# Storing attention outputs untransposed, adding their two shares by DMA, and normalising the stored rows later, in a hybrid attention and retention layer

## The chip, the cores and the metric

The kernel runs on one core of a Trainium2 chip, in float32. The metric is the device time of one launch in microseconds (us). Five engines work side by side, each on its own queue of instructions in order: TensorE (PE; its weight loads are shown as PEld), VectorE (DVE), ScalarE (ACT), GpSimd (POOL) and SyncE (SP), which here only issues DMAs. ScalarE and GpSimd issue DMAs too.

## What is computed

One layer on 1024 latent tokens (a grid of 16 rows by 64 columns) and 256 context tokens, width 1024. After adaptive normalisation one projection feeds two branches: neighbourhood attention with 8 heads of 64, and a two-way chunked retention with 4 heads. Both are projected, gated, merged, and followed by an output projection and a convolutional MLP. The part that matters here is the attention's output and its way into the projection:

```python
s_loc = jnp.einsum('bhqd,bhiqjd->bhqij', q_row, k_win) + bias[None]
...
s_ctx = jnp.einsum('bhqd,bhcd->bhqc', q_row, kc)
p = jax.nn.softmax(jnp.concatenate([s_loc, s_ctx], axis=-1).astype(jnp.float32), axis=-1).astype(v.dtype)
...
return (jnp.einsum('bhqij,bhiqjd->bhqd', p_loc, v_win)
        + jnp.einsum('bhqc,bhcd->bhqd', p_ctx, vc))
...
merged = jax.nn.sigmoid(gate_na) * (o_na @ w_proj_na) + jax.nn.sigmoid(gate_ret) * (o_ret @ w_proj_ret)
```

## The kernel before, in words

**Arithmetic.** Matmul operands are split into a high and a low part (float32r), and a product is the sum of three matmuls: high x high, high x low, low x high. `split` (lines 88 to 90) makes the parts: a cast on ScalarE, a subtraction on VectorE. `chain` (lines 105 to 117) runs such products and yields after every few matmuls, so that its caller can put them in pieces between other work.

**Order of the work.** The program is written engine by engine in program order; a scheduler with a model of durations then fixes the order on each engine, taking earlier lines first where several are ready, so that later work moves up into gaps. What is wrapped in `late` keeps its program order on its engine. Buffers come from pools: a tile with `bufs=n` has n places, and a new one waits until an old one is no longer used.

**Attention (80 to 376 us of the profile).** Heads are taken in 4 pairs, the queries of a pair in 8 blocks of 128 (a block is 16 grid rows by 8 columns, so tokens are stored grouped by block): 32 units. The loop over units overlaps three steps of neighbouring units. For unit i it issues `scores` (lines 470 to 490): eight matmuls, the maxima on VectorE, the exponentials with their sums on ScalarE, the reciprocals of the sums on VectorE into the unit's small tile `st`. For unit i-1 it transposes the probabilities on TensorE (`ptp`, lines 498 and 505), splits them (`PT`), and multiplies them with the values (`R`, line 516). The values stand as high and low columns, so `R` holds, for each head, 64 rows of the high values' share and 64 rows of the low values' share, with queries along the free axis; lines 518 and 519 add the shares of the probabilities' two parts into `rs`. For unit i-2 `output` (lines 522 to 531) transposes `rs` per head (`tq`), scales and adds the two value shares with the reciprocal (ACT line 528, DVE line 529) into `oq`, with queries as rows, and stores it by one SyncE DMA. Between these steps stand pieces of the next pairs' projections and of gate matmuls (`piece`), which fill TensorE's waits. With each unit GpSimd issues a DMA that prepares sums of weights (`puts`, line 587, and lines 555 and 559).

**Retention (376 to 690 us).** Four heads, each with 2 context blocks and 8 token blocks. A slot (`slot`) does one block's projection for one head (`front`, `turn`, `state`) and one mixing step of the head before (`mix_a`, `mix_b`, `mix_c`). `mix_a` splits the states, the high part on ScalarE (line 1203) and the low part on GpSimd (line 1204), and TensorE needs both. GpSimd goes on issuing the weight-sum DMAs, one or two a slot. SyncE loads the heads' weights (line 94) into a few buffers.

**Start of the merge (from 690 us).** SyncE loads the attention's rows back (`onr`, line 1366), 8 loads of 128 tokens by 512 channels. TensorE transposes them (`tpn`, line 1371, 32 transposes), ScalarE and VectorE split the result into `ona` (lines 1373 and 1374), and the projection `pn` (`mm_a` over `ona`, lines 113 to 115) follows, whose result is gated and stored. Beside it GpSimd and VectorE form sums of the normalised input for later gate matmuls (`b`, lines 1354 and 1357), in buffers that they share with `onr` (10 places).

The later parts, gates, output projection and MLP, are not touched.

Of the kernel before, what the change touches and what calls it, by code (L numbers as in the profile page):

```python
# [8 lines left out]
F32 = mybir.dt.float32  # L9
# [7 lines left out]
P = 128  # L17
# [8 lines left out]
NJ = 8  # L26
# [14 lines left out]
def tile_hybrid_layer(ctx, tc: tile.TileContext, io, dbg=None):  # L41
# [7 lines left out]
        return tc.alloc_tile_pool(name=name, bufs=bufs, side=side, space=PSUM, reuse_waits="tile")  # L49

    dram = tc.alloc_tile_pool(name="dram", bufs=1, space=DRAM)
    d_ona = dram.tile([GR, NJ, 8, NPAIR * P], F32, name="d_ona")
    d_oret = dram.tile([RH * 2, P, T], F32, name="d_oret")
    d_x1 = dram.tile([T, D], F32, name="d_x1")
    d_ada = dram.tile([32, P], F32, name="d_ada")
    d_s = dram.tile([6, 4, P, 512], F32, name="d_s")
    d_g = dram.tile([8, 4, P, 512], F32, name="d_g")
# [23 lines left out]
    pool.memset(mhalf, -0.5)  # L81

    col = cpool.tile([P, 48], F32, name="col")


    wpool = sb("wstream", "left")
# [41 lines left out]
    def perm(ap, c):  # L128
        return ap.rearrange("p (j r c) -> p r j c", j=NJ, c=c)
# [328 lines left out]
    class Unit:  # L458
# [8 lines left out]
        def scores(self):  # L467
            j, nl, nt, k0, pair = self.j, self.nl, self.nt, self.g0 * P, self.pair
            boff = 0 if j == 0 else (640 if j == NJ - 1 else 256)
            sl = [pna.tile([P, 512], F32, tag="sl", bufs=2, name="sl") for _ in range(2)]  # L470
            sc = pna.tile([P, 2, 512], F32, tag="sc", bufs=1, name="sc")[:, :, :C]
            self.st = st = na.tile([P, 16], F32, tag="st", bufs=3, name="st")
            self.Pm = Pm = [na.tile([P, 640], F32, tag="P", bufs=2, name="P") for _ in range(2)]
            for h in range(2):
                q = pair.qS[h][:, j * P : (j + 1) * P]
                k, kl = pair.kH[h], pair.kL[h]
                pe.matmul(sl[h][:, :nl], q, k[:, k0 : k0 + nl], start=True, stop=False)
                pe.matmul(sl[h][:, :nl], q, kl[:, k0 : k0 + nl], start=False, stop=True)
                pe.matmul(sc[:, h], q, k[:, T:NK], start=True, stop=False)
                pe.matmul(sc[:, h], q, kl[:, T:NK], start=False, stop=True)  # L480
            for h in range(2):
                vec.tensor_tensor_reduce(out=Pm[h][:, :nl], in0=sl[h][:, :nl], in1=pair.bias[h][:, boff : boff + nl], op0=ALU.add, op1=ALU.max, scale=1.0, scalar=NEG, accum_out=st[:, h : h + 1])
            vec.tensor_reduce(st[:, 2:4], sc, op=ALU.max, axis=AX.X)
            vec.tensor_tensor(st[:, 4:6], st[:, 0:2], st[:, 2:4], ALU.max)
            vec.tensor_scalar(st[:, 6:8], st[:, 4:6], -1.0, None, ALU.mult)
            for h in range(2):
                act.activation(Pm[h][:, :nl], Pm[h][:, :nl], AF.Exp, bias=st[:, 6 + h : 7 + h], scale=1.0, accum_out=st[:, 8 + h : 9 + h])
                act.activation(Pm[h][:, nl:nt], sc[:, h], AF.Exp, bias=st[:, 6 + h : 7 + h], scale=1.0, accum_out=st[:, 10 + h : 11 + h])
            vec.tensor_tensor(st[:, 12:14], st[:, 8:10], st[:, 10:12], ALU.add)
            vec.reciprocal(st[:, 14:16], st[:, 12:14])  # L490

        def transp(self, part):
            if part == 0:
# [17 lines left out]
        def values(self):  # L511
            R = pna.tile([P, 2, 2 * P], F32, tag="pt", bufs=2, name="R")
            for h in range(2):
                for c in range(self.nch):
                    g = self.g0 + c if c < self.ng else NJ + c - self.ng
                    pe.matmul(R[:, h], self.pair.V[:, g, h].rearrange("p a b -> p (a b)"), self.PT[h][:, c].rearrange("p a b -> p (a b)"), start=c == 0, stop=c == self.nch - 1)  # L516
            self.rs = rs = na.tile([P, 2, P], F32, tag="rs", bufs=1, name="rs")
            act.copy(rs, R[:, :, P : 2 * P])
            vec.tensor_tensor(rs, R[:, :, 0:P], rs, ALU.add)

        def output(self):
            tq = pna.tile([P, 4, 2, HD], F32, tag="pt", bufs=2, name="tq")
            for h in range(2):
                pe.transpose(tq[:, h].rearrange("p a b -> p (a b)"), self.rs[:, h], ident)
            oq = na.tile([P, 2, HD], F32, tag="oq", bufs=2, name="oq")
            for h in range(2):
                r = self.st[:, 14 + h : 15 + h]
                act.activation(oq[:, h], tq[:, h, 1], AF.Copy, scale=r)
                vec.scalar_tensor_tensor(oq[:, h], tq[:, h, 0], r, oq[:, h], ALU.mult, ALU.add)
            pr = self.pair.pr  # L530
            sync.dma_start(d_ona[:, self.j, :, pr * P : (pr + 1) * P], oq.rearrange("p a b -> p (a b)"))

    def ada_load():
        w = na.tile([P, D], F32, tag="aw", bufs=2, name="aw")
# [117 lines left out]
    with tc.manual_schedule():  # L652
# [302 lines left out]
        for shape, dt, tag, bufs in (  # L955
            ([P, 896], F32, "bias", 2),
            ([P, 16], F32, "st", 3),
            ([P, 640], F32, "P", 2),
            ([P, NJ + NCB, 2, 2, HD], F32R, "V", 1),
            ([P, 5, 2, P], F32R, "PT", 2),  # L960
            ([P, 2, P], F32, "rs", 1),
            ([P, 2, HD], F32, "oq", 2),
            ([P, 512], F32, "gs", 1),
        ):
            na.tile(shape, dt, tag=tag, bufs=bufs, name=tag)
# [77 lines left out]
        next(pieces, None)  # L1043

    us = []
    for i in range(NPAIR * NJ + 2):
        live = i < NPAIR * NJ
        u1 = us[i - 1] if 1 <= i <= NPAIR * NJ else None
        u2 = us[i - 2] if i >= 2 else None
# [12 lines left out]
        if u1:  # L1062
            u1.transp(1)
        if live:
            pair = pairs[i // NJ]
            if i % NJ == 0 and i:
                pair.load_bias()
            us.append(Unit(pair, i % NJ))
            us[i].scores()
        if u2:  # L1070
            u2.output()
        if u1:
            u1.values()
            puts(gate_sums, u1.st[:, 14:15], 1)
        piece()
        piece()
    for _ in pieces:
        pass
    pna.release()
    na.release()  # L1080
    csp.release()
# [7 lines left out]
    Dm = rc.tile([P, RH, P], F32, name="Dm")  # L1089

    def decay_masks():
        dtab = rt.tile([P, 4, P], F32, tag="dtab", bufs=1, name="dtab")
        sync.dma_start(dtab, io["dtab"])
        for h in range(RH):
            f, b = lg[:, 0, h : h + 1], lg[:, 1, h : h + 1]
            e1 = rt.tile([P, P], F32, tag="A0", bufs=1, name="e1")
            act.activation(e1, dtab[:, 0], AF.Exp, scale=f)
            act.activation(Dm[:, h], dtab[:, 1], AF.Exp, scale=b)
            vec.scalar_tensor_tensor(e1, e1, RKS, dtab[:, 2], ALU.mult, ALU.mult)
            vec.scalar_tensor_tensor(Dm[:, h], Dm[:, h], RKS, dtab[:, 3], ALU.mult, ALU.mult)  # L1100
            vec.tensor_tensor(Dm[:, h], Dm[:, h], e1, ALU.add)
# [161 lines left out]
            return self.n >= NTB + 2  # L1263


    def slot(main, mix, head=None, i=None):
        def step():
            next(main, None)
# [22 lines left out]


    mix, last = None, (None, None)
    for h in range(RH):
# [51 lines left out]
    d_onat = d_ona.rearrange("r j c d -> (r j c) d")  # L1346


    def hx_sums(k):
# [11 lines left out]
        yield  # L1361

    onr = []
    for n in range(KB):
        raw = g_raw("onr")
        sync.dma_start(raw, d_onat[n * P : (n + 1) * P])
        onr.append(raw)
    for n, raw in enumerate(onr):
        tp = pg.tile([P, NPAIR, P], F32, tag="g", bufs=6, name="tpn")
        for k in range(NPAIR):  # L1370
            pe.transpose(tp[:, k], raw[:, k * P : (k + 1) * P], ident)
        dst = [ona[w][:, :, n * P : (n + 1) * P] for w in range(2)]
        act.copy(dst[0], tp)
        vec.tensor_tensor(dst[1], tp, dst[0].bitcast(F32), ALU.subtract)


    def open3(out, ah, al, bh, bl, first, last):
# [741 lines left out]
```

## Time and profile before

| | us |
|---|---|
| median of 3 runs (1734.2 to 1735.79) | 1734.36 |
| the profiled execution, first to last instruction | 1733.2 |
| TensorE busy in it | 1717.1 |
| VectorE busy in it | 1222.2 |
| ScalarE busy in it | 839.6 |
| GpSimd busy in it | 540.4 |

The profile gives for each engine the time in which it was busy; a matmul's end is modelled, so matmuls overlap and a busy TensorE need not be at its peak. A row of a view names a source line, an engine, an operation, what is written from what, and a count. A wait row names the instruction that waited, what it waited for, and then the total, the count and the longest. The chain of work that ended last is followed back from the last instruction, at each step to what released it, or to the instruction before it on its engine. SPq and ACTq rows are DMA issues on SyncE and ScalarE. Issue rows of the DMA view end with the size and the median time from issue to landing; queue rows give packets, MB, and the time of their packets as a share of 16 DMA engines over the span.

### The profile page before, as it was taken

The numbers are of one execution on the slowest core, as the hardware profiler recorded it, in microseconds if no ns is written. First come the engines' busy times: TensorE is split into PE (matmuls) and PEld (weight loads), VectorE is DVE, ScalarE is ACT, GpSimd is POOL, SyncE is SP. The second block draws the span as 40 slices with busy tenths as digits, with TensorE's granted clock in tenths as the row PEclk, the third lists the DMA queues.
The fourth block names the chain that finished last, engine by engine and source line by source line (L and its number), as shares of the span: only waits on it lengthen the run. The fifth ranks groups of instructions, "written<-read, shape, count | busy, mean of one in ns | idle before, by whom it ended". The sixth has DMA issues, their size and how long they took to land.

```text
span 1733.2 us, 25367 instructions
## 1 busy us (share of the span) xinstructions
PE 1717.1 (99%) x8552; PEld 1435.8 (83%) x8552; DVE 1222.2 (71%) x2461; ACT 839.6 (48%) x1796; POOL 540.4 (31%) x706
## 2 busy tenths in 40 slices
PE   9999999999999999999999999999999999999997
PEld 7788888888888888888888888788788888888886
DVE  5778787665676766855555657867888889856756
ACT  6566666563453434543444333644444444545444
POOL 2100000002334343512223121012667667311444
PEclk9999999999999999999999999999999999999999
DMA  9344455532231223588975656768666776998744
GB/s 378 95 138 143 141 158 160 151 118 64 68 101 37 77 46 109 180 273 256 277 241 201 217 184 181 272 216 230 172 165 179 196 192 168 261 313 294 242 153 175
DMA packets 142002, 313.04 MB, mean 181 GB/s; under 512 B 19152, under 2 KB 32112, under 8 KB 135664
## 3 DMA queue, kind: packets, MB, share of 16 engines
q1 hardware_dynamic: 117536, 230.40, 38.6%
q0 software_dynamic: 12032, 70.27, 18.1%
q10 hardware_dynamic: 12304, 10.75, 1.8%
q8 instruction: 67, 1.10, 0.2%
q14 instruction: 63, 0.52, 0.1%
HBM read 250.78 MB, written 121.91 MB: 215 GB/s over the span
## 4 chain that ended last, share of the span: by engine, by line
PE 81%; issue 5%; DMA 5%; DVE 5%; POOL 2%; ACT 2%; SPq 0%; POOLq 0%; ACTq 0%; DVEq 0%
PE u L1379 28%; PE mm L126 4%; PE mm L124 4%; PE mm L125 4%; PE mm L115 4%; PE mm L114 4%; PE mm L113 4%; PE y L1379 2%; PE R L516 2%; DMA ur<-d_a 2%; PE pr L114 2%; PE pr L113 2%; PE pr L115 2%; PE ptp L498 2%; PE om L125 1%
## 5 line engine op out<-in xcount | busy, mean ns | idle before, releaser
L1379 PE MATMUL u<-T,wc 128*128 128x512 f32 x960 | 225.3, 390 | 0.7 <-ACT pu L1413 0.5
L1379 PEld LDWEIGHTS u<-T,wc 128*128 128x128 f32 x960 | 179.4, 188 | 40.9 <-ACT pu L1413 3.7
L1379 PE MATMUL y<-wc,ahl 128*128 128x512 f32 x924 | 210.1, 389 | 0.4 <-DVE wc L90 0.4
L1379 PEld LDWEIGHTS y<-wc,ahl 128*128 128x128 f32 x924 | 173.3, 188 | 36.8 <-DVE wc L90 0.8
L90 DVE TENSOR_TENSOR wc<-ur,wc 128x512 fp32r<-128x512 f32 x161 | 119.2, 743 | 62.6 <-ACT wc L89 60.8
L89 ACT CAST wc<-ur 128x512 fp32r<-128x512 f32 x161 | 99.7, 621 | 117.7 <-PE u L1379 74.1
L114 PE MATMUL mm<-low,wc 128*128 128x512 f32 (+1 forms) x312 | 118.9, 381 | 0.0
L1379 PE MATMUL u<-h2a,wc 128*128 128x512 f32 x480 | 113.1, 390 | 0.4 <-DVE pu L1422 0.4
L113 PE MATMUL mm<-hx,wc 128*128 128x512 f32 x264 | 107.4, 407 | 0.3 <-ACT hc L227 0.3
L1379 PEld LDWEIGHTS u<-h2a,wc 128*128 128x128 f32 x480 | 89.7, 188 | 20.5 <-issue 1.5
L115 PE MATMUL mm<-hx,wc 128*128 128x512 f32 x264 | 105.3, 399 | 0.0
L1379 PE MATMUL u<-hxT,wc 128*128 128x512 f32 x384 | 89.6, 389 | 0.0
L587 POOL COPY pad<-pu 128x1 f32<-128x1 f32 x54 | 36.6, 678 | 163.2 <-DVE pu L1416 120.9
L587 POOL COPY pad<-st 128x1 f32<-128x1 f32 x32 | 5.9, 185 | 257.7 <-DVE st L490 257.7
L1379 PEld LDWEIGHTS u<-hxT,wc 128*128 128x128 f32 x384 | 72.1, 188 | 14.9
L89 ACT CAST wc<-raw 128x512 fp32r<-128x512 f32 x86 | 53.1, 621 | 43.6 <-PE pr L115 9.2
L126 PE MATMUL mm<-wc,low 128*128 128x512 f32 (+1 forms) x180 | 68.9, 383 | 0.0
L89 ACT CAST wc<-s 128x512 fp32r<-128x512 f32 x56 | 34.8, 622 | 70.3 <-PE u L1379 70.3
L90 DVE TENSOR_TENSOR wc<-raw,wc 128x512 fp32r<-128x512 f32 x86 | 61.0, 713 | 9.5 <-ACT wc L89 8.8
L114 PEld LDWEIGHTS mm<-low,wc 128*128 128x128 f32 x312 | 59.0, 189 | 7.0
L1379 PE MATMUL u<-hx,wc 128*128 128x512 f32 x192 | 61.9, 390 | 0.0
L90 DVE TENSOR_TENSOR ahl<-ur,ahl 128x512 fp32r<-128x512 f32 x66 | 52.3, 800 | 11.8 <-ACT ahl L89 11.7
(412 smaller groups left out, 4731.3 us busy)
## 6 DMA issues: line engine op xcount, KB each, us to landing
d_a<-at SPq DMA_DIRECT2D x77, 256.0 KB, 6.1
ur<-d_a SPq DMA_DIRECT2D x77, 256.0 KB, 5.3
ur<-in_w_up SPq DMA_DIRECT2D x74, 256.0 KB, 5.9
d_w<-in_w_down POOLq DMA_DIRECT2D x66, 256.0 KB, 7.3
aw<-in_w_ada SPq DMA_DIRECT2D x32, 512.0 KB, 3.6
d_a<-d_a POOLq DMA_DIRECT2D x44, 256.0 KB, 7.4
ur<-d_w SPq DMA_DIRECT2D x44, 256.0 KB, 3.8
d_s<-in_w_up POOLq DMA_DIRECT2D x36, 256.0 KB, 6.1
```

The costliest lines, as they stand in the source:

```text
L89: act.copy(hi, src)
L90: (lo_eng or vec).tensor_tensor(lo, src, hi.bitcast(F32), ALU.subtract)
L113: pe.matmul(out, wh, xh, start=k == 0, stop=False)
L114: pe.matmul(out, wh, xl, start=False, stop=False)
L115: pe.matmul(out, wl, xh, start=False, stop=k == n - 1)
L124: pe.matmul(out, ah, bh, start=first, stop=False)
L125: pe.matmul(out, ah, bl, start=False, stop=False)
L126: pe.matmul(out, al, bh, start=False, stop=last)
L498: pe.transpose(tp[:, c], self.Pm[h][:, c * P : (c + 1) * P], ident)
L516: pe.matmul(R[:, h], self.pair.V[:, g, h].rearrange("p a b -> p (a b)"), self.PT[h][:, c].rearrange("p a b -> p (a b)"), start=c == 0, sto ...
L587: late(pool.tensor_copy(tick, src))
L1379: pe.matmul(out, a, b, start=first and n == 0, stop=last and n == 2, skip_group_check=True)
```

## The change

In the attention a unit is finished one step earlier. `rs` is stored as it is, 64 rows by two heads by 128 queries, by one SyncE DMA for each value share, into `d_ona[pair, share, channel, token]`; the transposes `tq`, the scalings and `oq` are gone, `rs` has two buffers, and the loop has one iteration less. The reciprocals go to a constant tile `rcol`, are transposed once after the last unit and stored as rows in `d_r`.

In the retention a new generator `shares` first adds the low share to the high share in DRAM, by four accumulating GpSimd DMAs of 512 KB in the first head's last four slots. Then, in the token slots of heads 1 and 2, it takes the sums in eight pieces of 128 channels by 512 tokens: in one slot it loads the piece and the reciprocals' rows (a broadcast for each head of the pair), in the next it multiplies on VectorE and stores the piece back from ScalarE's queue. Multiply, store and accumulating DMAs keep their program order.

At the start of the merge the rows are already channels by tokens. `onr` is eight loads (4 pairs, 2 halves of the tokens) of 128 channels by 512 tokens, in runs of 64 elements, and the split into `ona` reads them in the order of tokens; there are no transposes. A tile of the decay masks moves to a tag that it shares with the pieces, and `d_g` is declared larger, with the same part of it in use.

```diff
-    d_ona = dram.tile([GR, NJ, 8, NPAIR * P], F32, name="d_ona")
+    d_ona = dram.tile([NPAIR, 2, P, T], F32, name="d_ona")
+    d_r = dram.tile([NPAIR, 2, T], F32, name="d_r")
...
-            vec.reciprocal(st[:, 14:16], st[:, 12:14])
+            vec.reciprocal(rcol[:, pair.pr, :, j], st[:, 12:14])
...
         def output(self):
-            tq = pna.tile([P, 4, 2, HD], F32, tag="pt", bufs=2, name="tq")
-            for h in range(2):
-                pe.transpose(tq[:, h].rearrange("p a b -> p (a b)"), self.rs[:, h], ident)
-            oq = na.tile([P, 2, HD], F32, tag="oq", bufs=2, name="oq")
-            for h in range(2):
-                r = self.st[:, 14 + h : 15 + h]
-                act.activation(oq[:, h], tq[:, h, 1], AF.Copy, scale=r)
-                vec.scalar_tensor_tensor(oq[:, h], tq[:, h, 0], r, oq[:, h], ALU.mult, ALU.add)
-            pr = self.pair.pr
-            sync.dma_start(d_ona[:, self.j, :, pr * P : (pr + 1) * P], oq.rearrange("p a b -> p (a b)"))
+            pr, cs = self.pair.pr, slice(self.j * P, (self.j + 1) * P)
+            for w in range(2):
+                o = d_ona[pr, w].rearrange("(h d) q -> d h q", h=2)[:, :, cs]
+                sync.dma_start(o, self.rs[w * HD : w * HD + HD])
...
-        if u2:
-            u2.output()
         if u1:
             u1.values()
-            puts(gate_sums, u1.st[:, 14:15], 1)
+            u1.output()
+            puts(gate_sums, u1.st[:, 12:13], 1)
...
+    rt_ps = pna.tile([P, 512], F32, tag="pt", bufs=2, name="rtp")
+    pe.transpose(rt_ps[: 2 * NPAIR * NJ, :P], rcol.rearrange("p a h j -> p (a h j)"), ident)
+    rrow = na.tile([P, 2, P], F32, tag="rs", bufs=2, name="rrow")
+    act.copy(rrow[: 2 * NPAIR * NJ, 0], rt_ps[: 2 * NPAIR * NJ, :P])
+    sync.dma_start(d_r.rearrange("a h (j q) -> (a h j) q", q=P), rrow[: 2 * NPAIR * NJ, 0])
...
+    def shares():
+        for pr in range(NPAIR):
+            late(pool.dma_start(d_ona[pr, 0], d_ona[pr, 1], accum_op=ALU.add, max_dma_last_dim=8192))
+            yield
+        for pr in range(NPAIR):
+            for half in range(2):
+                cs = slice(half * 512, half * 512 + 512)
+                o, r = (rt.tile([P, 512], F32, tag="nrm", bufs=2, name=n) for n in ("osum", "rrep"))
+                sync.dma_start(o, d_ona[pr, 0, :, cs])
+                for h in range(2):
+                    sync.dma_start(r[h * HD : h * HD + HD], d_r[pr, h : h + 1, cs].to_broadcast([HD, 512]))
+                yield
+                late(vec.tensor_tensor(o, o, r, ALU.mult))
+                late(act.dma_start(d_ona[pr, 0, :, cs], o))
+                yield
...
+            if (h == 0 and i >= NCB + 4) or (h in (1, 2) and i >= NCB):
+                next(share, None)
...
-    for n in range(KB):
-        raw = g_raw("onr")
-        sync.dma_start(raw, d_onat[n * P : (n + 1) * P])
-        onr.append(raw)
-    for n, raw in enumerate(onr):
-        tp = pg.tile([P, NPAIR, P], F32, tag="g", bufs=6, name="tpn")
-        for k in range(NPAIR):
-            pe.transpose(tp[:, k], raw[:, k * P : (k + 1) * P], ident)
-        dst = [ona[w][:, :, n * P : (n + 1) * P] for w in range(2)]
-        act.copy(dst[0], tp)
-        vec.tensor_tensor(dst[1], tp, dst[0].bitcast(F32), ALU.subtract)
+    for half in range(2):
+        for pr in range(NPAIR):
+            raw = g_raw("onr")
+            src = d_ona[pr, 0].rearrange("p (j x) -> p j x", j=NJ)[:, :, half * 64 : half * 64 + 64]
+            sync.dma_start(raw.rearrange("p (j x) -> p j x", j=NJ), src)
+            onr.append((pr, half, raw))
+    for pr, half, raw in onr:
+        dst = [ona[w][:, pr, half * 512 : half * 512 + 512].rearrange("p (r j c) -> p r j c", j=NJ, c=8) for w in range(2)]
+        act.copy(dst[0], perm(raw, 8))
+        vec.tensor_tensor(dst[1], perm(raw, 8), dst[0].bitcast(F32), ALU.subtract)
```

More of the change, by code (lines that the diff above doesn't have):

```diff
@@ L56, in tile_hybrid_layer @@
     d_s = dram.tile([6, 4, P, 512], F32, name="d_s")
-    d_g = dram.tile([8, 4, P, 512], F32, name="d_g")
+    d_g = dram.tile([RH + KB, 4, P, 512], F32, name="d_g")
     d_gate = dram.tile([2 * KB, 2, P, 512], F32, name="d_gate")
@@ L83, in tile_hybrid_layer @@
     col = cpool.tile([P, 48], F32, name="col")
+    rcol = cpool.tile([P, NPAIR, 2, NJ], F32, name="rcol")
     wpool = sb("wstream", "left")
@@ L516, in values @@
                     pe.matmul(R[:, h], self.pair.V[:, g, h].rearrange("p a b -> p (a b)"), self.PT[h][:, c].rearrange("p a b -> p (a b)"), start=c == 0, stop=c == self.nch - 1)
-            self.rs = rs = na.tile([P, 2, P], F32, tag="rs", bufs=1, name="rs")
+            self.rs = rs = na.tile([P, 2, P], F32, tag="rs", bufs=2, name="rs")
             act.copy(rs, R[:, :, P : 2 * P])
@@ L960, in tile_hybrid_layer @@
             ([P, 5, 2, P], F32R, "PT", 2),
-            ([P, 2, P], F32, "rs", 1),
-            ([P, 2, HD], F32, "oq", 2),
+            ([P, 2, P], F32, "rs", 2),
             ([P, 512], F32, "gs", 1),
@@ L1045, in tile_hybrid_layer @@
     us = []
-    for i in range(NPAIR * NJ + 2):
+    for i in range(NPAIR * NJ + 1):
         live = i < NPAIR * NJ
-        u1 = us[i - 1] if 1 <= i <= NPAIR * NJ else None
-        u2 = us[i - 2] if i >= 2 else None
+        u1 = us[i - 1] if i >= 1 else None
         if i == 0:
@@ L1091, in decay_masks @@
     def decay_masks():
-        dtab = rt.tile([P, 4, P], F32, tag="dtab", bufs=1, name="dtab")
+        dtab = rt.tile([P, 4, P], F32, tag="nrm", bufs=2, name="dtab")
         sync.dma_start(dtab, io["dtab"])
@@ L1293, in tile_hybrid_layer @@
     mix, last = None, (None, None)
+    share = shares()
     for h in range(RH):
@@ L1345, in tile_hybrid_layer @@
     ona = [onap.tile([P, NPAIR, T], F32R, name=f"ona{i}") for i in range(2)]
-    d_onat = d_ona.rearrange("r j c d -> (r j c) d")
     def hx_sums(k):
```

## The prediction

> **What bounds the kernel now.** I read the page first: span, busy times, and the shares of the chain of work that ended last.
>
> ```profile
> span 1733.2 us, 25367 instructions
> ...
> PE 1717.1 (99%) x8552; PEld 1435.8 (83%) x8552; DVE 1222.2 (71%) x2461; ACT 839.6 (48%) x1796; POOL 540.4 (31%) x706
> ...
> PE 81%; issue 5%; DMA 5%; DVE 5%; POOL 2%; ACT 2%; SPq 0%; POOLq 0%; ACTq 0%; DVEq 0%
> ```
>
> TensorE is in the chain for 81% of the span and hardly ever idle, so the first question about any edit is how much TensorE time it takes out or puts in. The runs have a median of 1734.36 us, 1.2 us above this execution's span; I sum against the span and add 1.2 at the end.
>
> Next the table by stage. The change touches three: the neighbourhood attention (80 to 376 us), the retention (376 to 690), and the start of the merge, where the attention rows are read back (690 to 712).
>
> ```profile
> 80.00:376.00 296.00, 294.92 (x1819) 257.62 (x1818) 225.46 (x635) 190.02 (x559) 26.77 (x67) 1.00 0.48 143
> 376.00:690.00 314.00, 313.17 (x1655) 268.66 (x1654) 206.27 (x698) 133.31 (x382) 112.92 (x186) 1.00 0.28 74
> 690.00:712.00 22.00, 21.55 (x114) 17.41 (x113) 17.63 (x29) 11.89 (x24) 14.47 (x12) 1.00 0.68 210
> ```
>
> The columns after the length are the busy times of matmul, weight load, VectorE (DVE), ScalarE (ACT) and GpSimd (POOL), then the granted clock, the DMA share and GB/s. In the first two stages TensorE is idle for 1.1 and 0.8 us. VectorE stands at 225 of 296 us in the attention, the closest second. The granted clock is 1.00 in all three, so no time hides there.
>
> **The attention.** Per unit (one pair of heads, one block of 128 queries; 32 units) the old `output` makes two transposes `tq`, two ACT scalings, two DVE multiply-adds and one store. The chain within the stage, by line, and one unit of it in order of time:
>
> ```profile
> by line: PE mm L115 16.3%; PE mm L114 16.3%; PE mm L113 16.1%; PE R L516 11.3%; PE ptp L498 9.5%; PE sl L478 3.1%; PE sl L477 3.1%; PE tq L524 2.4%; PE sc L479 2.4%; PE sc L480 2.3%; PE ptp L505 1.7%; DMA aw<-in_w_ada 1.6%; PE vtp L446 1.6%
> ```
>
> ```profile
> 336.15 0.12 PE sc L480
> 336.27 0.22 PE tq L524 x2
> 336.49 0.24 PE mm L113
> ```
>
> The two transposes hold TensorE for 0.22 us, although a matmul row would show some 0.27 us for each: matmuls overlap, and start-to-start time is what counts. 32 pairs of 0.22 us are 7.0 us; the 2.4% of 296 us gives 7.1. I take 7.1 us out.
>
> Whether these come out of the span depends on what TensorE does next. In this stage projection and gate matmuls (`mm`, lines 113 to 115) fill every wait, and they are ready work: whatever slot `tq` leaves, the next such matmul takes. What stands against it are the waits that TensorE does have:
>
> ```profile
> PEld ptp L498 <- ACT P L487: 3.0, 8, 0.8
> ...
> PEld R L516 <- DVE PT L509: 1.7, 6, 0.3
> ```
>
> The second is the value matmul `R` waiting for the last piece of the transposed probabilities. `tq` stands just ahead of `R` and covers part of that latency; without it `R` may simply wait 0.22 us longer, where no `mm` is put between. That bounds the gain from below at 0. The other way, the engines that make these inputs lose work:
>
> ```profile
> L528 ACT ACTIVATE oq<-tq,st x64: 308/315/330, 109.3 to 375.0; 128x64 f32<-128x64 f32 x64
> L529 DVE SCALAR_TENSOR_TENSOR oq<-tq,st,oq x64: 262/275/285, 110.6 to 375.3; 128x64 f32<-128x64 f32 x64
> L531 SPq DMA_DIRECT2D d_ona<-oq x32: 524/530/643, 111.5 to 375.6; - x32
> ```
>
> That is 64 x 0.315 = 20.2 us of ScalarE and 64 x 0.275 = 17.6 us of VectorE. Both are off the path, so by themselves they give nothing; at best they remove the two waits above, 4.7 us. I count 0, and keep 0 to 11.8 us for the stage, with 7.1 taken because TensorE is in the chain almost throughout.
>
> The new stores are two per unit instead of one. SyncE's issue of one took 0.53 us; 64 of them make 34 us in a stage of 296, with weight and bias loads behind them. Each now waits for `rs` (line 519) directly instead of for `oq` one unit later, and `rs` has two buffers. Nothing on TensorE reads what they write, so I count 0. The one transpose and ScalarE copy of the reciprocals at the end add 0.1 us on TensorE, half of a `tq` pair; with the empty last iteration gone the matmuls of the first retention head follow as before. I put +0.2.
>
> **The start of the merge.** Here the chain leaves TensorE's steady stream:
>
> ```profile
> 701.18 0.26 PE mm L115
> 701.48 0.46 issue
> 701.94 0.63 ACT wc L89
> 702.60 1.17 DVE wc L90
> 703.77 0.61 DVE ona L1374
> 704.43 1.25 PE tpn L1371 x8
> 705.71 0.47 PE pn L113
> ```
>
> ```profile
> 701.26 2.78 PE L1371 MATMUL tpn<-ident,onr 128*128 128x128 f32 x24
> ```
>
> ```profile
> L1373 ACT CAST ona<-tpn x8: 588/626/671, 702.5 to 705.8; 128x512 fp32r<-128x512 f32 x8
> L1374 DVE TENSOR_TENSOR ona<-tpn,ona x8: 673/673/676, 703.7 to 707.9; 128x512 fp32r<-128x512 f32 x8
> ```
>
> From the first read-back transpose (701.26) to the first projection matmul `pn` (705.71) pass 4.45 us. All 32 transposes go. The eight casts and eight subtractions stay, from SBUF instead of PSUM. If they run ahead of 701.26, which they now may because they need neither TensorE nor a bank, the whole 4.45 us goes. If they stay where they are, `pn` can start at 702.5 + 0.63 = 703.1 with the high parts, then follows VectorE: low parts from 704.4 at 0.67 us each, the fourth at 706.4, the chain of twelve over at about 707.1. Before, twelve matmuls of some 0.24 us from 705.71 end near 708.6. So the gain is 1.5 to 4.45 us; I take 3.0, the middle, since space for `ona` may or may not be free early.
>
> The loads that feed this are now rows of 256 bytes (1,024 a load) instead of 2 KB. No row here shows such a load. The nearest are the queues:
>
> ```profile
> q1 hardware_dynamic: 117536, 230.40, 38.6%
> ...
> q10 hardware_dynamic: 12304, 10.75, 1.8%
> ```
>
> ```profile
> d_g<-d_g POOLq DMA_DIRECT2D x16, 256.0 KB, 4.1
> ...
> d_oret<-ot ACTq DMA_DIRECT2D x32, 128.0 KB, 1.9
> ...
> onr<-d_ona SPq DMA_DIRECT2D x8, 256.0 KB, 4.0
> ```
>
> ```profile
> 687.07 8.94 SPq L1366 DMA_DIRECT2D onr<-d_ona  x8
> ```
>
> Shares of 16 x 1733.2 engine-us: 10,704 us for 230.40 MB on q1 and 499 us for 10.75 MB on q10, 46 us per MB either way, though q10 holds the 512-byte rows of `d_oret` (4.2 of its MB). At that rate 256 KB over 16 engines take 0.76 us; at double the price eight take 12 us. In the trace they began at 687.07, 14 us before they were used, so they still land in time or nearly so: 0 in the sum, up to 2 us late in the range.
>
> **The retention.** New here: four accumulating DMAs of 512 KB, issued by GpSimd in the first head, and in heads 1 and 2 eight pieces, each with three SyncE loads, one 128x512 VectorE multiply, and a store on ScalarE's queue. Nearest rows:
>
> ```profile
> L1357 DVE TENSOR_TENSOR b<-b x16: 676/684/1772, 708.5 to 739.4; 128x512 f32<-128x512 f32 x16
> ```
>
> ```profile
> 680.21 0.45 ACTq L1242 DMA_DIRECT2D d_oret<-ot  x1
> ```
>
> ```profile
> L1232 DVE TENSOR_SCALAR o<-o,mvr x32: 411/414/3434, 450.1 to 696.0; 128x256 f32<-128x256 f32 x32
> ```
>
> ```profile
> 695.95 0.80 POOL L555 DMA_DIRECT2D d_g<-d_g  x1
> ...
> 696.03 3.43 DVE L1232 TENSOR_SCALAR o<-o,mvr 128x256 f32<-128x256 f32 x1 [0.73 <-POOL mvr L1231]
> ...
> 696.56 2.75 POOL L1354 TENSOR_TENSOR b<-hx,low 128x512 f32<-128x512 f32 x2
> ```
>
> Eight multiplies of 0.684 are 5.5 us, eight store issues of 0.45 are 3.6 us, four GpSimd issues of 0.80 are 3.2 us: 12.3 us if all of it reached TensorE, 0 if none did. The multiply and the store keep their program order, so behind a multiply on VectorE stand the next slot's rotary products and splits, and behind a store waiting for it on ScalarE the next value casts and state casts; TensorE waits for both about a slot later. TensorE was idle in the stage for only 0.8 us of 314 while VectorE stood at 66% and ScalarE at 42%, so most of this is covered. I take 1.5 us. The accumulating DMAs themselves are off the path: one of 256 KB landed in 4.1 us, so four of 512 KB take some 33 us one after another, and the first piece, of pair 0, is loaded six slots of 6 us after pair 0's own.
>
> The last two rows show a price beyond that: a VectorE operation with a median of 0.414 us was stretched to 3.43 while GpSimd ran two operations on SBUF, and the maximum of the 128x512 row is 1.772 us against a median of 0.684. I leave this out of the sum, since it hit few operations, and take it up as a rival.
>
> Sum: -7.1 - 3.0 + 0.2 + 1.5 = -8.4 us; span 1724.8, median 1726.0.
>
> **Rivals.** *More relief.* If both waits in the attention go and the read-back casts run early: -11.8 - 4.4 + 0.2 + 1.5 = -14.5, so 1719.9. For it: VectorE's load there; against: those waits are short and scattered over some fourteen places.
>
> *No gain in the attention.* `R` waits for its probabilities as long as `tq` lasted: -3.0 + 0.2 + 1.5 = -1.3, so 1733.1. For it: the wait of `R`; against: it occurs 6 times, not 32, and in the excerpt `mm` already stands between `tq` and `R`.
>
> *Multiplies that collide with GpSimd.* Each of the eight meets a state split on GpSimd and takes the row's maximum, 1.09 us more, and TensorE is held for all of it: -8.4 + 8.7 = +0.3, so 1734.7. For it: the two stretched operations above; against: GpSimd works 113 us of the stage's 314, so some three of eight would meet, and not all of that would be exposed. [...]
>
> *Slower: the shared queues hold VectorE in the retention.* SyncE serves in order, and behind a weight load whose buffer isn't free it stands long:
>
> ```profile
> SPq L94 <- DVE kz L1173: 169.1, 7, 60.5
> ```
>
> ```profile
> d_ona<-oq SPq DMA_DIRECT2D x32, 64.0 KB, 2.0
> ```
>
> If a piece's loads come behind such a load, or wait for the previous piece's store to leave its buffer (2.0 us to land), the multiply holds VectorE in its program order and TensorE behind it. With x us per piece the result is -9.9 + 8x: no gain from x = 1.2, slower by over 0.2% from 1.7. At 2.0 it is +6.1, so 1740.5. Against it: a whole slot (314 us over some 50 slots, 6 us) lies between a piece's loads and its multiply.
>
> **How the numbers follow.** About 0.2% (3.5 us) is what a measurement here can tell from no change. Chances: forecast 0.57, more relief 0.14, no gain in the attention 0.12, collisions 0.05, held queues 0.12. The first two are faster: 0.71; the next two the same: 0.17; the last slower: 0.12. Range 1719 to 1735: from just below the larger gain to just above the collisions; left out are the slower case and a little below and above.
>
> **What would show it.** Right: no `tq`, `oq`, `tpn` rows; the stretch from the first value transpose to the last `R` some 7 us shorter; `pn` 0 to 2 us after the last gate matmul, with its casts ahead of it; multiplies near 0.7 us and TensorE's waits in the retention up by no more than 2 us. Wrong: waits of `R` grown by some 7 us; a retention longer by over 5 us with TensorE released by DVE or ACT late behind the multiply; `pn` waiting for the read-back loads; or a stage that the change doesn't touch longer by several us.

## The result and the profile after

The changed kernel takes **1739.36 us** (median of 18 runs, 1735.15 to 1741.29); the kernel before 1734.38 us (18 runs, 1732.68 to 1735.83). The ratio is 1.0028, 95% interval 1.0021 to 1.0035. The forecast was 1726.0, with 71% on faster. It is slower by 5.0 us. One launch of e6 below (2854.1 us, at a granted clock of 0.56) was slow as a whole and is left out of e6's median, which would be 1739.44 us with it.

The profiled execution of after took 1738.33 us, with a span of 1736.6 us (before: 1733.2). First the page: span, TensorE and the chain's shares by engine.

```profile
span 1736.6 us, 25162 instructions
...
PE 1713.1 (99%) x8457; PEld 1425.9 (82%) x8457; DVE 1223.9 (70%) x2405; ACT 824.6 (47%) x1733; POOL 548.2 (32%) x710
...
PE 77%; DVE 6%; issue 6%; DMA 4%; POOL 3%; ACT 2%; SPq 0%; POOLq 0%; ACTq 0%; DVEq 0%
```

TensorE has 4.0 us less work, and yet the span is longer; its share of the chain fell from 81 to 77%. So the loss is not in the amount of matmul work, and the table by stage of after says where it is:

```profile
80.00:376.00 296.00, 295.00 (x1787) 255.98 (x1786) 217.40 (x584) 180.02 (x511) 26.77 (x67) 1.00 0.55 155
376.00:690.00 314.00, 307.95 (x1614) 261.97 (x1614) 207.90 (x693) 127.48 (x366) 118.94 (x189) 1.00 0.37 94
690.00:712.00 22.00, 19.58 (x78) 13.63 (x76) 16.89 (x24) 11.10 (x22) 12.35 (x12) 0.87 0.87 215
```

The attention is as full as before. In the retention TensorE is now idle for 6.05 us instead of 0.83, with a DMA share of 0.37 instead of 0.28, and at the start of the merge it is idle more and its granted clock is 0.87 instead of 1.00.

A few marks, read from the two traces (start of the instruction named, us), locate the losses. `dS` is the retention's state product; its 216 matmuls are counted here in 12 groups of 18, and a group's mark is its first matmul.

| mark | before | after | difference |
|---|---|---|---|
| last `R` of the attention | 372.6 | 365.6 | -7.0 |
| `dS` group 3 | 418.6 | 411.6 | -7.0 |
| `dS` group 4 | 441.9 | 438.9 | -3.0 |
| `dS` group 6 | 490.0 | 487.6 | -2.4 |
| `dS` group 8 | 539.7 | 540.0 | +0.3 |
| last gate matmul ahead of the projection | 701.0 | 702.1 | +1.1 |
| first projection matmul `pn` | 705.7 | 704.2 | -1.5 |
| last projection matmul `pn` | 749.4 | 754.2 | +4.8 |

The attention gave its 7.0 us. Then 4.0 were lost between 412 and 439 us, 2.7 between 488 and 540, 1.4 in small pieces; 2.6 were won ahead of the projection, and 6.3 lost in it. From its first matmul to the last start of one the projection takes 50.0 us instead of 43.7. Later stages absorb 1.5 us of the 4.8, so that the two profiled spans differ by 3.3.

**Loss 1, 412 to 439 us.** TensorE's waits in the retention of after, whole stage:

```profile
PEld dS L126 <- ACT kz L1170: 6.7, 4, 2.3
PEld Q L127 <- POOL SS L1202: 0.8, 2, 0.5
```

The first is new; 3.9 us of it, in two waits, fall between 405 and 443 us. `kz` is a cast of ScalarE, and ScalarE, in order, stood behind casts of late weights (waits of ScalarE for the same work, before at 419 to 447 us and then after at 412 to 440):

```profile
ACT wx L89 <- DMA raw<-in_w_ret: 2.2, 1, 2.2
ACT wc L89 <- DMA raw<-in_w_ret: 2.1, 2, 1.6
```

```profile
ACT wx L91 <- DMA raw<-in_w_ret: 5.0, 2, 3.0
ACT wc L91 <- DMA raw<-in_w_ret: 5.0, 2, 4.5
```

The DMA view of 419 to 443 us, before and then after (count, KB each, median us to landing), shows who was in the way: two of the accumulating DMAs, beside the eight loads of the second head's weights.

```profile
raw<-in_w_ret SPq DMA_DIRECT2D x8, 256.0 KB, 3.5
```

```profile
raw<-in_w_ret SPq DMA_DIRECT2D x8, 256.0 KB, 5.8
d_ona<-d_ona POOLq DMA_DIRECT2D x2, 512.0 KB, 8.6
```

SyncE itself was not late with these loads, although it had stood 34.7 us at the first piece's load until an accumulating DMA had landed: the first of the eight is issued at 421.1 us in after and at 428.15 in before, the same 7 us that the attention gave. But the eight issues take 18.2 us instead of 12.6.

**Loss 2, 488 to 540 us.** SyncE's queue from 488 to 519 us, before and then after (start, us, instruction):

```profile
501.21 12.74 SPq L94 DMA_DIRECT2D raw<-in_w_ret  x8
```

```profile
491.66 0.33 SPq L1272 DMA_DIRECT2D osum<-d_ona  x1
495.16 1.80 SPq L1274 DMA_DIRECT2D rrep<-d_r  x2
498.93 4.85 SPq L96 DMA_DIRECT2D raw<-in_w_ret  x4
506.16 0.33 SPq L1272 DMA_DIRECT2D osum<-d_ona  x1
507.14 1.47 SPq L96 DMA_DIRECT2D raw<-in_w_ret  x2
510.08 1.82 SPq L1274 DMA_DIRECT2D rrep<-d_r  x2
512.01 4.24 SPq L96 DMA_DIRECT2D raw<-in_w_ret  x2
```

The eight weight loads of the third head, 12.7 us in one piece before, take from 498.9 to 516.3, with loads of the pieces in between. At these loads (L1272 and L1274) SyncE, in order, waits long, for VectorE and for the store of an earlier piece (490 to 545 us, after):

```profile
SPq L1272 <- DVE A L1210: 19.6, 1, 19.6
SPq L1272 <- DVE kz L1171: 10.4, 2, 7.8
SPq L1274 <- DMA d_ona<-osum: 9.8, 3, 5.2
```

TensorE's largest wait between 486 and 520 us of after, where before has none, is again for the cast `kz`:

```profile
PEld dS L126 <- ACT kz L1170: 2.3, 1, 2.3
```

**Loss 3, the projection.** The split of the read-back rows in after (ns minimum/median/maximum, first and last start):

```profile
L1388 ACT CAST ona<-onr x8: 614/617/618, 703.5 to 707.2; 128x512 fp32r<-128x512 f32 x8
L1389 DVE TENSOR_TENSOR ona<-onr,ona x8: 684/1762/1784, 704.3 to 713.9; 128x512 fp32r<-128x512 f32 x8
```

and, in order of time, TensorE up to the first two `pn`, VectorE and GpSimd (three excerpts):

```profile
702.12 0.39 PE L117 MATMUL mm<-hx,wc 128*128 128x512 f32 x1
704.22 0.50 PE L115 MATMUL pn<-ona,wc 128*128 128x512 f32 x1 [1.71 <-ACT ona L1388]
705.03 0.50 PE L116 MATMUL pn<-ona,wc 128*128 128x512 f32 x1 [0.31 <-DVE ona L1389]
```

```profile
704.29 11.43 DVE L1389 TENSOR_TENSOR ona<-onr,ona 128x512 fp32r<-128x512 f32 x8
```

```profile
705.05 13.52 POOL L1370 TENSOR_TENSOR b<-hx,low 128x512 f32<-128x512 f32 x8 [4.64 <-DVE ona L1389]
```

The casts run back to back (eight in 4.26 us), so the 256-byte loads were in time. The casts begin at 703.5, not ahead of the last gate matmul: ScalarE came to them behind the copy `gs` of that matmul's result and a weight cast. The first `pn` comes 2.1 us after the last gate matmul (before: 4.7). But a subtraction takes 1.76 us where it took 0.67, all the while that GpSimd forms its sums (median 1.70 us each, before 1.40), and TensorE waits for one after the other:

```profile
PEld pn L116 <- DVE ona L1389: 6.0, 7, 1.2
```

### The profile page after: what moved, and what is told of

Same layout as the page of the kernel before. It is cut to its first block, busy times and chain, and to the rows that moved or that the text cites. A ratio compares the mean times of both kernels' runs of the same rounds, so it can differ in the third digit from the quotient of the medians.

```text
span 1736.6 us, 25162 instructions
## 1 busy us (share of the span) xinstructions
PE 1713.1 (99%) x8457; PEld 1425.9 (82%) x8457; DVE 1223.9 (70%) x2405; ACT 824.6 (47%) x1733; POOL 548.2 (32%) x710
## 4 chain that ended last, share of the span: by engine, by line
PE 77%; DVE 6%; issue 6%; DMA 4%; POOL 3%; ACT 2%; SPq 0%; POOLq 0%; ACTq 0%; DVEq 0%
PE u L1394 28%; PE mm L117 4%; PE mm L115 4%; PE mm L116 4%; PE mm L128 3%; PE mm L126 3%; PE mm L127 3%; PE y L1394 2%; PE R L518 2%; PE ptp L500 2%; DMA ur<-d_a 2%; PE pr L116 2%; PE pr L115 2%; PE pr L117 2%; PE om L127 1%
## 5 line engine op out<-in xcount | busy, mean ns | idle before, releaser
L1170 ACT ACTIVATE kz<-r,dec 128x128 fp32r<-128x128 f32 x72 | 27.9, 400 | 76.4 <-POOL r L1151 76.1
```

## The experiments

All are edits of the kernel after unless said otherwise; each was timed beside the kernel before. Three theories stood: **A**, the accumulating DMAs crowd the DMA engines while weights are loaded (loss 1); **B**, the pieces' loads stand ahead of weight loads in SyncE's order (loss 2); **C**, the subtractions, now with both operands in SBUF, and GpSimd's sums slow each other (loss 3). Rivals: A and B one cause; for loss 1, GpSimd's issuing of the DMAs, not their bytes, or SyncE held at the first piece's load; and for C, VectorE's load as such, or the strided read.

**e1: the accumulating DMAs four slots earlier.**

```diff
-            if (h == 0 and i >= NCB + 4) or (h in (1, 2) and i >= NCB):
+            if (h == 0 and NCB <= i < NCB + 4) or (h in (1, 2) and i >= NCB):
```

> The four accumulating DMAs move from the last four slots of the first head to its first four token slots; nothing else. Theory A (they crowd the weight loads of the next head on the DMA engines): those loads land in about 3.5 us again instead of a median of 5.8, TensorE's waits for the state casts in the retention fall from 6.7 to under 2 us, the first four of the eight lost microseconds come back, the last gate matmul before the projection moves from 702.1 to about 698, the time from 1739.4 to about 1735.4. Theory B (SyncE, held by the first piece's load, issues the weight loads late): their first issue stays at 421 and the time changes by less than 1 us. Theory C (the new instructions on VectorE, ScalarE and GpSimd cost the time themselves): no change.

Measured: 1735.32 us (ratio 1.0012, 1.0002 to 1.0022). `dS` group 4 starts at 435.3, 6.6 us earlier than before; group 8 at 536.1 (3.6 earlier), so loss 2 is left. The weight loads at 419 to 443 us land in 4.2 us. Loss 1 comes with the place of these four DMAs. The first of the weight loads is issued at 421.6 us, no earlier than in after (421.1), so it was not SyncE's hold that made them late.

**e12: the accumulating DMAs in their place, a sixteenth of their bytes** (the other low shares are left out of the sum).

```diff
-            late(pool.dma_start(d_ona[pr, 0], d_ona[pr, 1], accum_op=ALU.add, ...))
+            late(pool.dma_start(d_ona[pr, 0, :, :64], d_ona[pr, 1, :, :64], accum_op=ALU.add, ...))
```

> The four accumulating DMAs stay in their slots on GpSimd's queue but move only the first 64 of 1,024 columns (32 KB instead of 512 KB each; the other low shares are left out of the sum). Theory (their bytes crowd the DMA engines while the second head's weights are loaded): loads of weights back to a median landing of 3.5 to 4.2 us there, the fourth group of dS at 435.5 us instead of 438.9, time down by some 3 to 4: 1735 to 1736. Rival (GpSimd's issues, 0.8 to 1.1 us each, hold up its rotary products and with them ScalarE's casts of k): the issues are unchanged, so no gain, 1738.5 to 1740, landings aside.

Measured: 1736.14 us (1.0009, 1.0000 to 1.0018), `dS` group 4 at 435.4. The DMA view of 419 to 443 us of e12:

```profile
raw<-in_w_ret SPq DMA_DIRECT2D x8, 256.0 KB, 3.7
...
d_ona<-d_ona POOLq DMA_DIRECT2D x2, 32.0 KB, 5.1
```

GpSimd issues as many DMAs in the same slots, SyncE is held at the first piece's load nearly as long (32.7 us) and issues the first weight load at 421.7, the weights land in time again, and loss 1 is gone: it is the bytes, not the issuing or the hold.

**e2: the pieces' loads behind the weight loads,** in program order (`late`), and the pieces in other slots.

```diff
-                sync.dma_start(o, d_ona[pr, 0, :, cs])
+                late(sync.dma_start(o, d_ona[pr, 0, :, cs]))
...
-            if (h == 0 and i >= NCB + 4) or (h in (1, 2) and i >= NCB):
+            if (h == 0 and i >= NCB + 4) or (h == 1 and NCB <= i < NCB + 6) or (h == 2 and i >= NCB) or (h == 3 and NCB <= i < NCB + 2):
```

(The loads of `rrep` likewise.)

> The pieces' loads are kept in program order on SyncE and no step of a piece falls into the last two slots of the second head, so that its loads stand behind the third head's weight loads and not between them; the last piece moves to the fourth head. Theory B for the second loss (about 2.4 us near 500 us of the trace): the eight weight loads there are issued within about 12.5 us as before, instead of 17.0, the step between the third and the fourth head is as short as before, the time falls by 2 to 2.5 us to about 1737. Theory A alone: no change there, since the accumulating DMAs are long done. Theory C: no change.

Measured: 1736.92 us (1.0015, 1.0006 to 1.0024), 2.4 less than after. SyncE's queue in e2, same window:

```profile
499.82 0.34 SPq L96 DMA_DIRECT2D raw<-in_w_ret  x1
500.26 0.38 SPq L1272 DMA_DIRECT2D osum<-d_ona  x1
500.69 1.09 SPq L1274 DMA_DIRECT2D rrep<-d_r  x2
501.94 11.60 SPq L96 DMA_DIRECT2D raw<-in_w_ret  x7
```

Seven of the eight go out in one piece again, TensorE has no wait between 486 and 520 us, and groups 4 to 8 of `dS` keep one lead of 1.3 to 1.4 us over before: loss 2 is gone, loss 1 is not. Which of the two edits did it was not separated.

**e4: e1 and e2 together.**

> Both shifts of the retention together: the accumulating DMAs four slots earlier, and the piece loads behind the weight loads with no piece in the slots where the next head's weights are loaded. If the two losses are separate (crowded DMA engines at 412 to 439 us, SyncE's order at 490 to 515 us), they add: 1739.4 - 4.0 - 2.4 = 1733.0, and the last gate matmul comes near 695.5 us (after: 702.1; nothing of the pieces at all: 695.2), every group of dS 6 us earlier than before from the third on. If there is one cause with two names, the second shift brings no more than the first alone, 1735.3, last gate matmul near 697.8. The start of the merge is unchanged: eight subtractions near 1.5 us, projection some 50 us long.

Measured: 1732.12 us (0.9987, 0.9979 to 0.9996). The last gate matmul starts at 696.1. The gains add (4.0 + 2.4 off 1739.4 makes 1733.0), so A and B are two causes.

**e5: no shares at all** (the low shares are not added and the rows not normalised: accumulating DMAs, loads, multiplies and stores are left out).

> Leaves out the accumulating DMAs, the pieces' loads, the multiplies and the stores back: the value's low share is not added and the rows are not divided by the softmax sums. Theories A and B together: the retention gives back 6 to 6.5 us of its 8.1, last gate matmul at about 696. With C as well all 8.1 come back: last gate matmul at 694, the attention's 7 us kept to the end of the retention, time about 1731.3. The projection's stretch stays at 50 us under all of them.

Measured: 1730.72 us (0.9983, 0.9973 to 0.9992); the last gate matmul at 695.2. So the new work cost 8.6 us where 1.5 were forecast, and e4, with all that work in it, costs 1.4 more than e5. The projection still takes 50.0 us: loss 3 has nothing to do with the shares.

**e3: GpSimd's sums put off until the subtractions are done** (one small GpSimd copy that reads the last of them, ahead of the sums).

```diff
             hs = hx_sums(db // 2)
+            if db == 0:
+                late(pool.tensor_copy(tick, ona[1][:, NPAIR - 1, T - 1 : T].bitcast(F32)))
```

> GpSimd's first sum of the normalised input waits for the last split of the attention rows (one tiny copy ahead of it); nothing else. Theory L (VectorE's subtraction, whose operand moved from PSUM to SBUF, is shut out by GpSimd's sums): the eight subtractions take 0.68 us instead of a median of 1.76, the projection's span shrinks from 50.0 to about 44, and the time falls by about 6 us to about 1733. Theory D (the read-back loads with 256-byte runs come late): the subtractions' waits and the projection stay as they are, and the time does not change.

Measured: 1741.01 us (1.0043, 1.0028 to 1.0058), slower than after: a miss. The subtractions, TensorE's largest wait in the merge, and GpSimd in e3:

```profile
L1389 DVE TENSOR_TENSOR ona<-onr,ona x8: 684/690/693, 706.6 to 710.8; 128x512 fp32r<-128x512 f32 x8
```

```profile
PEld pn L115 <- DVE pnt L1530: 5.3, 3, 2.7
```

```profile
711.75 18.66 POOL L1370 TENSOR_TENSOR b<-hx,low 128x512 f32<-128x512 f32 x12
```

Half of C held: without the sums beside it a subtraction takes 0.69 us. But twelve sums then run in a row, and VectorE's later work is stretched instead (`hxT` 0.96 us a piece, in after 0.85); it gets to the projection's results (`pnt`) late, TensorE waits for it, and the projection takes 50.8 us. The collision had been moved, not removed. (2.3 us of this execution's loss lie in the retention, whose instructions e3 leaves alone; the last section returns to it.)

**e6 and e11: the subtraction from PSUM again.** ScalarE copies the loaded rows to a PSUM bank, and cast and subtraction read the bank.

```diff
-        act.copy(dst[0], perm(raw, 8))
-        vec.tensor_tensor(dst[1], perm(raw, 8), dst[0].bitcast(F32), ALU.subtract)
+        tp = pg.tile([P, 512], F32, tag="g", bufs=6, name="tpn")
+        act.copy(tp, raw)
+        act.copy(dst[0], perm(tp, 8))
+        vec.tensor_tensor(dst[1], perm(tp, 8), dst[0].bitcast(F32), ALU.subtract)
```

> ScalarE first copies each read-back row block into a PSUM bank, and cast and subtraction read the bank. Theory (GpSimd's sums shut out a subtraction with two SBUF operands, and that alone makes the projection long): subtractions back at 0.67 us, projection 44 to 45 us instead of 50.0; but some six copies of 0.6 us stand ahead of the first cast, so the first projection matmul comes 2 us later. Net -4: 1735 to 1736. Rival (the bound is all the two-operand work of VectorE beside GpSimd's sums, as the sums put off by the run before seemed to say): the wait moves to the results of the projection, which stays 49 to 51 us long, 1739 to 1742. Second rival (the strided read is slow by itself): the subtractions stay at 1.5 us, from PSUM too.

> The kernel whose subtractions read a PSUM copy once more, for its trace: its median was 1739.4, no gain over after. Theory: subtractions 0.67 us, but the first projection matmul some 4 us later behind ScalarE's copies, and the sums and the other two-operand work still collide, so that the projection's released results are late; together 8 us. Rival: subtractions still stretched to 1.5 us, the operand's place being no cause.

Measured: 1738.95 us (eight runs, 1735.23 to 1746.86; 1.0028, 1.0015 to 1.0042), no gain that can be told, where 1735 to 1736 was expected. e11 is the same kernel in one more execution (1733.12 us; its last gate matmul came at 698.5 instead of 702.1, and why is open):

```profile
L1391 DVE TENSOR_TENSOR ona<-tpn,ona x8: 680/681/692, 702.6 to 707.2; 128x512 fp32r<-128x512 f32 x8
```

```profile
PEld pn L115 <- DVE ona L1391: 6.1, 1, 6.1
```

With one operand in PSUM the subtraction takes 0.68 us, strided as it is, with GpSimd's sums going on beside it (GpSimd is busy in all of 700 to 708 us, a sum takes 1.41 us in the mean, in after 1.63): with e3, C is shown, and the strided read is not the cause. The projection shrinks to 45.7 us, but behind ScalarE's copies the first `pn` comes 6.1 us after the last gate matmul instead of 2.1. The two cancel: 51.8 us from gate to the last `pn`, against 52.1. The expectation for e6 had 2 us for those copies; they cost 4.

**e7 and e8: the sums on VectorE,** the first eight (e7) or all sixteen (e8).

```diff
-            late(pool.tensor_tensor(t, hxp(0, kb, c0, 512)...
+            late((vec if k < 2 else pool).tensor_tensor(t, hxp(0, kb, c0, 512)...
```

(In e8 `vec` throughout.)

> The first eight of the sixteen sums at the start of the merge are made by VectorE (0.68 us each) instead of GpSimd (1.63 us each). GpSimd is then idle during the subtractions. Theory (mutual exclusion): subtractions 0.7 us, projection 44 to 46 us, 1734 to 1736. Rival (VectorE's own queue becomes the bound, 5.4 us more on it): projection 48 us or longer with waits on its released results, 1738 or more.

> All sixteen sums on VectorE. Nothing is left for GpSimd to read beside the projection, so by the theory no VectorE operation there is stretched: every 128x512 row near 0.68 us, VectorE busy 10.9 us more for the sums and some 12 us less for stretched rows, projection 44 to 46 us, 1734 to 1736, level with the half or better. Rival (VectorE full): waits on the projection's released results of 3 us or more, 1737 to 1740, slower than the half.

Measured: 1733.69 (1.0000, 0.9991 to 1.0009) and 1733.31 us (0.9995, 0.9985 to 1.0004), 5.7 and 6.1 less than after. VectorE's groups in e8, 696 to 762 us (busy us, mean ns):

```profile
L1373 DVE TENSOR_TENSOR b<-b 128x512 f32<-128x512 f32 x16 | 10.9, 684 | 0.0
L92 DVE TENSOR_TENSOR hxT<-b,hxT 128x512 fp32r<-128x512 f32 x16 | 10.6, 686 | 0.0
L1370 DVE TENSOR_TENSOR b<-hx,low 128x512 f32<-128x512 f32 x16 | 10.1, 685 | 0.0
```

Every row is back at 0.68 us (in after `b` averaged 0.86 and `hxT` 0.85, the sums on GpSimd 1.63). With the eight subtractions these rows take VectorE 36.5 us, sums included; in after they took 38.3 without the sums. The projection takes 44.0 us. VectorE was not full; its rows had been stretched beside GpSimd's sums.

**e9: the shifts of e4 and the sums of e8.**

> The two shifts of the retention and all sixteen sums of the merge on VectorE. If the three losses are separate, the gains add once more: 1732.1 (both shifts alone) - 6.0 (the sums alone, 1739.4 to 1733.3) = 1726.1, the last gate matmul near 696 us, the projection 44 us long. Rival: the later stage soaks up part of it (in the expansion, y, before's lead of the projection was already half lost in some runs), or VectorE is full, 1728 to 1730.

Measured: **1726.86 us** (5 runs, 1724.53 to 1727.22; 0.9954, 0.9941 to 0.9966). The three losses are separate, and this version beats both kernels. Its chain:

```profile
PE 84%; issue 5%; DMA 4%; DVE 3%; POOL 2%; ACT 1%; SPq 0%; POOLq 0%; ACTq 0%; DVEq 0%
```

**e10: the kernel before with its sums on VectorE,** a control.

> The kernel before, with the sixteen sums on VectorE: a control. Theory (the sums cost only where VectorE has two-operand SBUF work that TensorE waits for; before's subtractions read PSUM and its projection, 43.7 us long, had no wait): no change, 1733.5 to 1735. Rival (the sums on VectorE are a gain of their own that the change's trouble only hid): 1729 to 1732.

Measured: 1733.41 us (0.9996, 0.9987 to 1.0005): no change that can be told. The projection takes 43.7 us as in before. So the move of the sums is worth 6 us only with the change; it repairs what the change broke.

## Why the prediction was wrong

- **Attention, -7.1: right.** The last `R` comes 7.0 us earlier, `tq` is gone, and the matmuls behind filled the place; `R` waited hardly longer (2.5 us in all, 1.9 before).
- **Empty last iteration and reciprocals, +0.2: right;** the first `dS` still leads by 7.0.
- **Retention, +1.5: wrong in kind and size.** It gave back 8.1 in the profile, 8.6 by e5. The step that failed: "The accumulating DMAs themselves are off the path". I had asked only when their results were needed. They needed nothing in time, and their bytes made others late: a weight load landed after 5.8 us instead of 3.5, ScalarE's casts waited behind one another, and TensorE with them (4.0; e1, e12). What I did price, 12.3 us of multiplies and issues at 1.5, is not the loss: e4 keeps all of it, in other slots, and lies 1.4 us above e5. The multiplies took 1.13 us in the median instead of 0.68, and no wait of TensorE names them.
- **The held queues: the slower rival was near in time (1740.5), with half a mechanism, so its nearness is luck.** It had SyncE's queue, but the wrong way round: pieces late behind weight loads, holding VectorE. On the chip the pieces' loads stood ahead of weight loads and made those late (2.7 in the profile; e2 won 2.4). It had no crowding, and not the larger loss in the projection.
- **Start of the merge, -3.0: the gap right, the rest wrong.** The gap from gate matmul to projection shrank by 2.6, and the loads of 256 bytes came in time, landing after 5.0 us in the median (before 4.0; the double price allowed for them was my assumption); SyncE took 1.09 us for each issue instead of 0.38, with no wait to show for it. But the 3.0 was the middle of two cases, and the worse one happened: the casts stayed behind, and the first `pn` came at the 703.1 foreseen for it, plus the 1.1 by which the gate matmul was late; for that case the prediction had a gain of 1.5. The step that failed: "The eight casts and eight subtractions stay, from SBUF instead of PSUM", with 0.67 us kept. The operand's new place, beside GpSimd's sums, was the price: 1.76 us a piece, and 6.3 on the projection (e3, e11). I had the 1.772 us row of this very stage, and weighed it only against the eight new multiplies, in a stage where GpSimd has gaps (113 of 314 us busy). What the runs show of it: with one operand in PSUM a subtraction takes 0.67 and 0.68 us beside the running sums (before, e11); with both in SBUF 1.76 beside them (after) and 0.69 without them (e3).
- **The sum:** -7.1 was measured as -7.0, +1.7 as +8.1, -3.0 as +3.7; -8.4 became +4.8 at the end of the projection, +3.3 in the profiled span, and the median +5.0; the profiled execution of after was 1.0 us faster than its median. With the three losses repaired (e9) the time is 1726.9.

## What to carry to other kernels

A DMA whose result is needed late is not free (here two of 512 KB beside eight weight loads took these from 3.5 to 5.8 us): look at what else is loaded in the same 20 us, and whether those loads have slack, and put bulk traffic where the trace shows the DMA engines empty. On a shared in-order queue ask both who waits behind the new load and who is now ahead of the urgent one (eight weight issues took some 17 us instead of 12.7). When an edit moves an operand from PSUM to SBUF, cost every instruction that reads it again, beside what GpSimd does at that moment (0.67 us became 1.76); and if engines collide, moving the work to the faster engine can beat moving it in time (a sum took 0.69 us on VectorE and 1.63 on GpSimd; e8 took 1733.31 us, e3 1741.01).

## What the hardware showed that was not expected

After a short stall of TensorE its granted clock was lower in some executions and not in others. Granted clock is the third number from the right. First after (its stalls lie between 702 and 714 us), then e9 (its stall is at 695 to 697):

```profile
704.00:708.00 4.00, 3.15 (x9) 1.83 (x10) 4.00 (x5) 3.81 (x8) 2.95 (x2) 0.77 0.44 138
708.00:712.00 4.00, 3.93 (x9) 1.92 (x7) 4.00 (x3) 2.29 (x3) 4.00 (x4) 0.50 0.40 127
712.00:716.00 4.00, 2.78 (x8) 1.44 (x8) 4.00 (x4) 0.14 (x1) 4.00 (x3) 0.87 0.00 2
```

```profile
696.00:700.00 4.00, 2.67 (x7) 1.87 (x8) 3.52 (x6) 4.00 (x9) 0.00 (x0) 0.75 0.62 216
700.00:704.00 4.00, 4.00 (x16) 3.26 (x15) 4.00 (x8) 2.10 (x4) 0.00 (x0) 0.82 0.36 131
```

In e8, with the same gap of 2.1 us, the clock stayed at 1.00, and its projection took 44.0 us; those of e7 and e9, with a drop (to 0.57 and 0.75 in 4 us), took 45.6, which is 1.6 us more (e9 has the sums of e8; e7 has half of them still on GpSimd). Where TensorE waits for VectorE anyway the drop cost nothing: the projections of e1 and e5 (clock 1.00) and of after and e4 (down to 0.50 and 0.53) all take 50.0 us. The retention shows a drop too, with the same instructions; after first, then e8:

```profile
518.00:524.00 6.00, 6.00 (x31) 5.00 (x31) 3.78 (x12) 2.24 (x7) 2.31 (x4) 1.00 0.03 9
```

```profile
518.00:524.00 6.00, 6.00 (x25) 4.90 (x24) 3.98 (x12) 2.89 (x9) 2.18 (x4) 0.77 0.12 41
```

TensorE is busy throughout in both, yet e8 gets 25 matmuls through where after has 31, and from `dS` group 7 to 8 it takes 26.1 us instead of 24.5. e3 does as e8 (clock 0.72, 26.1 us), which makes up most of its loss in the retention. Here the wait just ahead was longer as well, 3.1 us in e8 and 2.9 in e3 against 2.3 in after; but e12 has a drop (0.73 from 512 to 518 us) behind a wait of 2.3, and e1 none (1.00) behind one of 2.5. Ahead of the projection e8 and e9 both have the gap of 2.1 us and a wait of 0.6 us right behind it, e8 without a drop, e9 with one. So the length of the wait alone does not decide it, and what does was not shown. Such drops may also be why after spreads over 6.1 us and before, which hardly stalls, over 3.2; that was not tried by itself.
